# Scaling attention weights on GpSimd and placing the compression units one unit later in a two-layer trunk

## The chip, the core and the metric

The kernel runs on one core of a Trainium2 chip. The metric is the device time of one execution in microseconds. The engines of a core are named as in the profile: PE (TensorE, matrix products and transposes), DVE (VectorE), ACT (ScalarE), POOL or Pool (GpSimd) and SP (SyncE, which issues the transfers from memory).

## What is computed

A trunk of two layers over 256 positions of width 1,024. Each layer adds three branches to the stream. The first mixes positions: eight query heads of width 64 in two groups attend to keys in three ways (compressed blocks, selected blocks, a sliding window), and beside them runs a retention with four heads. The other two are an MLP and a gated input.

```python
def nsa_mixer(q_in, kc_in, vc_in, ks_in, vs_in, kw_in, vw_in, gate_logits, ...):
    q = rmsnorm(q_in.reshape(B, S, G, Hg, dh).transpose(0, 2, 3, 1, 4), qn_g)
    ...
    k_cmp = rmsnorm(compress(k_c, pos_k, w1_k, w2_k), kn_g)
    v_cmp = compress(v_c, pos_v, w1_v, w2_v)
    ...
        p_cmp = masked_softmax(s, cmp_end[None, :] <= t[:, None])
        o_cmp = jnp.einsum('bghqn,bgnd->bghqd', p_cmp.astype(dtype), v_cmp)
    ...
        return gc[..., 0:1] * o_cmp + gc[..., 1:2] * o_slc + gc[..., 2:3] * o_win

def reference(x, p, ...):
    for i in range(DEPTH):
        h = rmsnorm(x, norm_mix[i])
        z = h @ w_in[i]
        ...
        y_a = nsa_mixer(...) @ w_up_nsa[i]
        y_b = retention(rq, rk, rv, rg) @ w_up_ret[i]
        mix = jax.nn.sigmoid(merge_a) * y_a + jax.nn.sigmoid(merge_b) * y_b
        x = x + mix @ w_out[i]
        h = rmsnorm(x, norm_mlp[i])
        x = x + jnp.square(jax.nn.relu(h @ w_ff1[i])) @ w_ff2[i]
        gate = jax.nn.sigmoid(rmsnorm(x, norm_ple[i]) @ w_ple_gate[i])
        x = x + gate * (p[i] @ w_ple[i])
    return x
```

With 256 positions all blocks are selected, so the selected branch is a full causal attention.

## The kernel before

**Units of weight.** A layer's weights come in 142 units of 128 partitions by 1,024 numbers (512 KB). The string ORDER names the first 45 of them in the order in which PE uses them: kcvc and ksvs (keys and values), kvg (window keys, values and gates), q, rq, rk, rv, rg (retention), and w0 to w7 (the first matrix of the compressor). `fa` and `fb` stand for the two halves of the row norm. `_plan` adds the merge, output, MLP and gate units. SP loads each unit into a ring of four buffers `raw`; the units w lie in four other buffers. ACT rounds a unit to its high half `hi` (line 188), and DVE subtracts to get the low half `lo` (line 192). Both have six buffers, and a unit is split four units before its use (AHEAD = 4). PE multiplies three times: high by high, high by low, low by high. One unit is 24 matmuls of 128x256 or 12 of 128x512; a unit w is four matmuls of 128x512.

**Order.** PE's order is that of the program text. Between the matmuls of a unit the program pokes generators (`kv_tail`, `q_tail`, `compress`, `attend` with `softmax` and `scores`, `collect` with `weigh` and `retain`), which emit their instructions when a model clock `vt` says that their inputs should be there. `charge` advances that clock by costs written in the code: for Pool 0.14 us and a microsecond for every 310 elements of a row (a pow: 1.1 or 2.6). A generator yields the model time at which it wants to go on. The order of DVE, ACT and Pool follows a scheduler's priorities. A change in any cost therefore moves instructions on all engines.

**Front of a layer.** `windows` builds the overlapping windows ZB of the compressor's input (DVE `zt`, `zs`, ACT and DVE `ZB`); w0 to w7 multiply them into one accumulator `ot`. `compress` then applies a selection matmul (`pt<-cst,tmp`), a gelu and the second matrix. `kv_tail` norms and transposes keys into KT, `q_tail` transposes the queries into qT and computes the query factor `nq`, minus the product of the row norm `r` and the rsqrt of the head's squares (a pow on Pool, `rso`). All transposes and small products share two buffers `pt`.

**Attention.** Four times (group g, half t), `softmax` takes the scores `sc` of four heads through a mask operation on DVE (line 208, which multiplies by `nq`), an exponential on ACT and the factor `acf` (gate over sum). `weigh` multiplies each block of `e` by its column of `acf` on DVE (`scale`: two or four blocks of 4x128, one of 4x16), transposes the block on PE (`turn`, `pt<-cst,e`), splits it into `pp` or, for the narrow block, PC, and multiplies by V into the single buffer `ot` (`apply`). The last product is `ot<-PC,VC`. ACT and DVE then fold `ot` into `o`, and split that into NHh and NHl, which the units ua multiply. `retain` uses the same buffer `ot` for retention, takes the result through a pow on Pool, and transposes the normed rows (`pt<-cst,tmp`).

Of the kernel before, what the change touches and what calls it, by code (L numbers as in the profile page):

```python
# [12 lines left out]
ALU = mybir.AluOpType  # L13
AX = mybir.AxisListType

P = 128
# [6 lines left out]
NH = 8  # L23
# [22 lines left out]
for _n, _w in PAR_PARTS:  # L46
# [7 lines left out]


ORDER = (
# [4 lines left out]
)  # L61


# [31 lines left out]
def trunk(ctx: ExitStack, tc: tile.TileContext, xT, wu, wg, cst, msk, par, pin, out):  # L95
# [50 lines left out]
    vt = {"pe": 0.0, "act": 0.0, "dve": 0.0, "pool": 0.0}  # L146
    cur = [0.0]

    def width(ap):
        n = 1  # L150
        for d in ap.shape[1:]:
            n *= d
        return n
# [5 lines left out]
    def charge(eng, us):  # L159
        us += 0.03  # L160
        if first[0]:
            cur[0] += us + 0.6
            return
        gs = gaps[eng]
        while len(gs) > 1 and gs[0][1] < vt["pe"] - 6.0:
            gs.pop(0)
        for i, (a, e) in enumerate(gs):
            s = max(a, cur[0])
            if s + us <= e:
                new = []  # L170
                if s - a > 0.15:
                    new.append([a, s])
                if e - s - us > 0.15:
                    new.append([s + us, e])
                gs[i:i + 1] = new
                break
        vt[eng] = gs[-1][0]
        cur[0] = s + us + 0.06

    def fresh(t=None):  # L180
        cur[0] = vt["pe"] if t is None else t
# [27 lines left out]

    def gp(**k):  # L210
        n = width(k["out"])
        charge("pool", (1.1 if n <= 4 else 2.6) if k["op"] == ALU.pow else 0.14 + n / 310)
        return nc.gpsimd.tensor_tensor(**k)  # L213

# [156 lines left out]
    LB = 7.0  # L371
    SL = 0.0
    DE = 0.5
    SLACK = {"kv_tail": 4.0, "q_tail": 3.0, "compress": 0.3, "attend": 1.0, "collect": 0.0}

    def spawn(gen, paced=False):
# [1 line left out]

    def step(gen):
        fresh()  # L380
        if gen.__name__ == "compress":
            first[0] = True
            try:
                with tc.high_priority():
                    d = next(gen)
            finally:
                first[0] = False
        else:
            d = next(gen)
        if d == "now":  # L390
            return cur[0]
        return (cur[0] if d is None else d) + SLACK.get(gen.__name__, SL)

# [125 lines left out]
    def layer(l, st):  # L519
# [108 lines left out]
        def q_tail(t, pq):  # L628
            pv = pq.rearrange("p (h d) -> p h d", h=NH)
            qn = qns[:, t]  # L630
            sq = tmp([P, NH, DH])
            with tc.high_priority():
                act(qn[:, :, 0, :].bitcast(F32R), pv, AF.Copy)
                sub(qn[:, :, 1, :], pv, qn[:, :, 0, :])
                act(sq, pv, AF.Square, scale=r[:, t:t + 1])
            due = cur[0]
            ss = small([P, NH], "qss")
            reduce_sum(ss, sq)
            rs = rsqrt_rows(ss, P, NH, 1.0 / DH)
            pow_due = cur[0]  # L640
            yield due
            yield
            for hh in range(2):
                pt = p_tile([P, 4, P])
                for h in range(4):
                    flip(pt[:, h, :], qn[:, 4 * hh + h].rearrange("p a b -> p (a b)"),
                                        ident)
                act(qT[:, 4 * hh:4 * hh + 4, t * P:(t + 1) * P], pt, AF.Copy)
                if hh == 0:
                    yield vt["pe"]  # L650

            fresh(max(pow_due, vt["pe"]))
            ts(out=nq[:, t], in0=rs, scalar1=r[:, t:t + 1], scalar2=-1.0, op0=ALU.mult, op1=ALU.mult)
            done.add(("q", t))


# [40 lines left out]
        def weigh(g, t):  # L697
# [11 lines left out]

            def scale(i):  # L710
                o, w, b, _ = blocks[i]
                tt(out=e[:, :, o:o + w], in0=e[:, :, o:o + w],
                   in1=cf[:, :, b:b + 1].to_broadcast([P, HG, w]), op=ALU.mult)

            def turn(i):
# [16 lines left out]
                mm(ot, vv, ph.rearrange("p a b -> p (a b)"), start=i == 0, stop=False)  # L732
                mm(ot, vv, pl.rearrange("p a b -> p (a b)"), start=False, stop=i == n)

            fin = []
            scale(0)
            scale(1)
            yield cur[0] + 1.5
            turn(0)
            fin.append(cur[0])  # L740
            yield vt["pe"]
            for i in range(1, n + 1):
                if i < n:
                    fresh(vt["pe"])
                    scale(i + 1)
                fresh()
                turn(i)
                fin.append(cur[0])
                yield fin[i - 1]
                apply(i - 1)  # L750
# [152 lines left out]
                act(ZB[:, :, s, 0, :], zs[:, s, :, :], AF.Copy)  # L903
                sub(ZB[:, :, s, 1, :], zs[:, s, :, :], ZB[:, :, s, 0, :].bitcast(F32))

        r = rh = rr = RB = None
        gk = small([P, 1], "gk")
        todo = set()

# [11 lines left out]
        for name, u in SEQ[l]:  # L921
# [7 lines left out]
            elif name == "fa":  # L929
                finish_a(st)  # L930
                r = st["r"]
                rh = small([P, 2], "rh")
                ts(out=rh, in0=r, scalar1=0.5, scalar2=None, op0=ALU.mult)
                rr = small([P, 2], "rr")
                tt(out=rr, in0=r, in1=r, op=ALU.mult)
                ready("fa")
# [382 lines left out]
```

## Time and profile before

| | us |
|---|---|
| three runs | 866.30, 864.49, 866.05 |
| median of the runs | 866.05 |
| the profiled execution | 865.38 |
| its span in the profile | 863.5 |
| PE busy in the span | 844.8 |
| DVE, ACT, Pool busy | 614.3, 500.7, 37.2 |

The span runs from the first to the last instruction of the profiled execution; the other 1.9 us of that execution lie around it. An engine's busy time says how much of the span it worked; idle time of an engine that nobody waits for costs nothing. Layer 0 takes about the first half of the span. Its front lies between about 20 and 75 us, its attention between 85 and 168 us; in layer 1 the front begins near 445 us and attention ends near 592 us.

### The profile page before, as it was taken

Reading aid. Unit: us, or ns where it says so; the run is one execution under the profiler, and the core shown is the slowest. Engines: PE = TensorE matmul, PEld = TensorE weight load, DVE = VectorE, ACT = ScalarE, POOL = GpSimd, SP = SyncE. Lnnn points to the kernel's source line nnn. Section 1 sums busy time; section 2 is a strip of 40 time slices with the busy share of each in tenths; the row PEclk is TensorE's granted clock in tenths of the full one; section 3 lists DMA queues with packets and bytes.
Section 4 is the critical chain, followed back from the end, with each engine's and each line's share of the span. In section 5 each row is a group of like instructions: output and inputs, shape, how many; then the busy total and the mean of one; then the engine's idle time right before and its main releaser. Section 6 shows DMA issues by size and latency. Waiting matters only on the chain.

```text
span 863.5 us, 16468 instructions
## 1 busy us (share of the span) xinstructions
PE 844.8 (98%) x6647; PEld 817.0 (95%) x6647; DVE 614.3 (71%) x1011; ACT 500.7 (58%) x836; POOL 37.2 (4%) x32
## 2 busy tenths in 40 slices
PE   8999999999999999999999999999999999999997
PEld 7888899899999999999998889998999999999997
DVE  6898897776955555557789879885968555555584
ACT  6786877444744444446576868663556444444461
POOL 1220000000000000000004000000000000000000
PEclk9999999999999999999999999999999999999999
DMA  7867354446556566566665644543556556556541
GB/s 256 314 224 228 123 163 134 137 126 187 190 177 187 183 192 178 190 183 220 188 197 169 200 144 146 172 139 100 158 178 195 178 190 180 187 185 183 194 123 49
DMA packets 44283, 152.10 MB, mean 176 GB/s; under 512 B 5168, under 2 KB 6960, under 8 KB 44208
## 3 DMA queue, kind: packets, MB, share of 16 engines
q1 hardware_dynamic: 44064, 151.04, 55.6%
q8 instruction: 52, 0.85, 0.4%
q14 instruction: 23, 0.19, 0.1%
q10 hardware_dynamic: 144, 0.01, 0.0%
HBM read 149.99 MB, written 1.05 MB: 175 GB/s over the span
## 4 chain that ended last, share of the span: by engine, by line
PE 87%; DVE 7%; ACT 2%; DMA 1%; issue 1%; POOL 1%; SPq 0%; DVEq 0%; ACTq 0%; POOLq 0%
PE mm L219 51%; PE sc L219 16%; PE pt L219 14%; PE ot L219 4%; DVE lo L192 3%; PE pt L224 3%; DMA raw<-in_wu_dram 1%; ACT hi L188 1%; POOL rso L213 1%; DVE zt L192 1%; DVE zs L192 0%; DVE gz L200 0%; DVE XT L192 0%; DVE qn L192 0%; DVE XL L200 0%
## 5 line engine op out<-in xcount | busy, mean ns | idle before, releaser
L192 DVE TENSOR_TENSOR lo<-raw,hi 128x1024 fp32r<-128x1024 f32 (+2 forms) x287 | 342.4, 1198 | 187.3 <-ACT hi L188 186.5
L188 ACT ACTIVATE hi<-raw 128x1024 fp32r<-128x1024 f32 (+2 forms) x287 | 296.4, 1039 | 278.9 <-PE mm L219 164.7
L219 PE MATMUL mm<-XH,hi 128*128 128x256 f32 x992 | 283.3, 286 | 0.0
L219 PE MATMUL mm<-XH,lo 128*128 128x256 f32 x992 | 279.6, 282 | 0.4 <-DVE lo L192 0.4
L219 PE MATMUL mm<-XL,hi 128*128 128x256 f32 x992 | 279.2, 281 | 0.0
L219 PEld LDWEIGHTS mm<-XH,hi 128*128 128x128 f32 x992 | 186.9, 188 | 0.9
L219 PEld LDWEIGHTS mm<-XL,hi 128*128 128x128 f32 x992 | 187.0, 188 | 0.6
L219 PEld LDWEIGHTS mm<-XH,lo 128*128 128x128 f32 x992 | 186.9, 188 | 0.6 <-DVE lo L192 0.6
L219 PE MATMUL sc<-ho,hi 128*128 128x256 f32 x512 | 96.8, 282 | 0.0
L219 PE MATMUL pt<-ho,hi 128*128 128x256 f32 x512 | 96.6, 281 | 0.0
L219 PEld LDWEIGHTS pt<-ho,hi 128*128 128x128 f32 x512 | 78.6, 188 | 0.0
L219 PEld LDWEIGHTS sc<-ho,hi 128*128 128x128 f32 x512 | 78.6, 188 | 0.0
L219 PE MATMUL pt<-ho,lo 128*128 128x256 f32 x256 | 72.0, 281 | 0.0
L219 PE MATMUL sc<-ho,lo 128*128 128x256 f32 x256 | 72.0, 281 | 0.0
L219 PEld LDWEIGHTS sc<-ho,lo 128*128 128x128 f32 x256 | 48.2, 188 | 0.0
L219 PEld LDWEIGHTS pt<-ho,lo 128*128 128x128 f32 x256 | 48.2, 188 | 0.0
L219 PE MATMUL mm<-hi,XH 128*128 128x512 f32 (+2 forms) x128 | 44.7, 349 | 0.0
L219 PE MATMUL mm<-lo,XH 128*128 128x512 f32 (+2 forms) x128 | 43.7, 341 | 0.2 <-DVE lo L192 0.2
L219 PE MATMUL mm<-hi,XL 128*128 128x512 f32 (+2 forms) x128 | 43.7, 341 | 0.0
L188 ACT ACTIVATE e<-e,nmx 128x128 f32<-128x128 f32 (+2 forms) x96 | 37.7, 396 | 9.1 <-DVE nmx L208 8.9
L213 POOL TENSOR_TENSOR rso<-rsv,mhalf 128x2 f32<-128x2 f32 (+3 forms) x18 | 28.2, 1576 | 289.8 <-DVE rsv L196 289.8
L208 DVE CUSTOM_DVE_ANT_0 e<-sc,masks,nq 128x128 f32<-128x128 f32 (+2 forms) x96 | 29.5, 351 | 1.6 <-PE sc L219 1.0
(189 smaller groups left out, 1333.0 us busy)
## 6 DMA issues: line engine op xcount, KB each, us to landing
raw<-in_wu_dram SPq DMA_DIRECT2D x275, 512.0 KB, 3.6
raw<-in_wg_dram SPq DMA_DIRECT2D x8, 280.0 KB, 4.2
cst<-in_cst_dram SPq DMA_DIRECT2D x1, 768.0 KB, 8.1
out_dram<-XT SPq DMA_DIRECT2D x3, 256.0 KB, 2.4
XT<-in_xT_dram SPq DMA_DIRECT2D x4, 128.0 KB, 2.8
raw<-in_wu_dram SPq DMA_DIRECT2D x4, 128.0 KB, 3.0
XT<-in_xT_dram SPq DMA_DIRECT2D x2, 256.0 KB, 6.5
tmp<-in_pin_dram SPq DMA_DIRECT2D x2, 256.0 KB, 3.7
```

The source lines that it names most:

```text
L188: return nc.scalar.activation(o, *a, **k)
L192: return nc.vector.tensor_tensor(**k)
L208: return nc.vector.tensor_tensor_reduce(**k)
L213: return nc.gpsimd.tensor_tensor(**k)
L219: return nc.tensor.matmul(o, a, b_, **k)
L224: return nc.tensor.transpose(o, a, i)
```

## The change

Four things. In ORDER each unit rq0 to rq3 moves ahead of the two units w that stood before it, in both layers. `scale` becomes a Pool multiply, and `weigh` issues all of them at its start; each `turn` is placed when the model has its scale done plus 3 us, where before the first turn came 1.5 us after two scales and each later one after the next scale. In `q_tail` the factor nq is a Pool multiply right behind the pow, by `rn`, which is minus `r` and a new small DVE operation at `fa`; before it was a DVE operation behind the transposes. The list AHEAD_OF_SPLITS names the generator that was named in the code before.

```diff
--- before.py
+++ after.py
@@ -54,10 +54,10 @@
 ORDER = (
-    "kcvc0 kvg0 kvg1 q0 sq kcvc1 kvg2 fa kvg3 q1 fb q2 q3 ksvs0 ksvs1 w0 w1 rq0 w2 w3 rq1 w4 w5  "
-    "rq2 w6 w7 rq3 rk0 rk1 rk2 rk3 rv0 rv1 rv2 rv3 rg0 rg1 rg2 rg3",
+    "kcvc0 kvg0 kvg1 q0 sq kcvc1 kvg2 fa kvg3 q1 fb q2 q3 ksvs0 ksvs1 rq0 w0 w1 rq1 w2 w3  "
+    "rq2 w4 w5 rq3 w6 w7 rk0 rk1 rk2 rk3 rv0 rv1 rv2 rv3 rg0 rg1 rg2 rg3",
...
@@ -637,7 +639,8 @@
             ss = small([P, NH], "qss")
             reduce_sum(ss, sq)
             rs = rsqrt_rows(ss, P, NH, 1.0 / DH)
-            pow_due = cur[0]
+
+            gp(out=nq[:, t], in0=rs, in1=rn[:, t:t + 1].to_broadcast([P, NH]), op=ALU.mult)
             yield due
             yield
             for hh in range(2):
@@ -648,9 +651,6 @@
                 act(qT[:, 4 * hh:4 * hh + 4, t * P:(t + 1) * P], pt, AF.Copy)
                 if hh == 0:
                     yield vt["pe"]
-
-            fresh(max(pow_due, vt["pe"]))
-            ts(out=nq[:, t], in0=rs, scalar1=r[:, t:t + 1], scalar2=-1.0, op0=ALU.mult, op1=ALU.mult)
             done.add(("q", t))
@@ -709,7 +709,7 @@
 
             def scale(i):
                 o, w, b, _ = blocks[i]
-                tt(out=e[:, :, o:o + w], in0=e[:, :, o:o + w],
+                gp(out=e[:, :, o:o + w], in0=e[:, :, o:o + w],
                    in1=cf[:, :, b:b + 1].to_broadcast([P, HG, w]), op=ALU.mult)
@@ -732,17 +732,17 @@
                 mm(ot, vv, ph.rearrange("p a b -> p (a b)"), start=i == 0, stop=False)
                 mm(ot, vv, pl.rearrange("p a b -> p (a b)"), start=False, stop=i == n)
 
-            fin = []
-            scale(0)
-            scale(1)
-            yield cur[0] + 1.5
+            fin, scaled = [], []
+            t0 = cur[0]
+            for i in range(n + 1):
+                fresh(t0)
+                scale(i)
+                scaled.append(cur[0] + 3.0)
+            yield scaled[0]
             turn(0)
             fin.append(cur[0])
-            yield vt["pe"]
             for i in range(1, n + 1):
-                if i < n:
-                    fresh(vt["pe"])
-                    scale(i + 1)
+                yield scaled[i]
                 fresh()
                 turn(i)
                 fin.append(cur[0])
...
@@ -931,6 +931,8 @@
                 r = st["r"]
                 rh = small([P, 2], "rh")
                 ts(out=rh, in0=r, scalar1=0.5, scalar2=None, op0=ALU.mult)
+                rn = small([P, 2], "rn")
+                ts(out=rn, in0=r, scalar1=-1.0, scalar2=None, op0=ALU.mult)
                 rr = small([P, 2], "rr")
                 tt(out=rr, in0=r, in1=r, op=ALU.mult)
                 ready("fa")
```


PE runs 5,791 rows in both programs, DVE 946 before and 923 now, Pool 38 and 58. The rows below give engine, operation and operands in the order in which an engine runs them; a number behind a name tells buffers of that name apart, and "..." stands for rows left out.

PE, layer 0, from the end of ksvs1 (`mm_493`) to rq0. Before, `hi_429` and `hi_452` are w0 and w1, `mm_600` is rq0:

```order
L219 MATMUL mm_493<-hi_393,XL_103 128x256
L219 MATMUL ot_580<-hi_429,ZB_166 128x512
L219 MATMUL ot_580<-lo_430,ZB_166 128x512
...
L219 MATMUL ot_580<-hi_452,ZB_166 128x512
...
L224 MATMUL pt_595<-cst,tmp_372 128x128 x2
L219 MATMUL mm_600<-XH_102,hi_496 128x256
```

There rq0 stands behind both units w and a pair of key transposes. Now `hi_431` is rq0, `hi_454` and `hi_500` are w0 and w1:

```order
L220 MATMUL mm_497<-hi_395,XL_103 128x256
L220 MATMUL mm_578<-XH_102,hi_431 128x256
...
L220 MATMUL mm_578<-XH_102,lo_432 128x256
L225 MATMUL pt_603<-cst,tmp_372 128x128 x2
...
L220 MATMUL ot_620<-hi_454,ZB_166 128x512
L220 MATMUL ot_620<-lo_455,ZB_166 128x512
...
L220 MATMUL ot_620<-hi_500,ZB_166 128x512
...
L225 MATMUL pt_635<-cst,tmp_383 128x128 x2
```

The 24 matmuls of rq0, with a pair of key transposes among them, now stand between ksvs1 and w0, and the other pair of transposes behind w1.

DVE, layer 0, first weighing, from the last mask operation of its fourth head. `e_1064`, `acf_1121` belong to this softmax, `e_1125` to the next:

```order
L208 ISA e_1064,nmx_1065<-sc_1112,masks,nq_170 128x128
...
L196 TENSOR_SCALAR acf_1121<-smx_1066 128x12
L693 RECIPROCAL acf_1121<-acf_1121 128x12
L192 TENSOR_TENSOR acf_1121<-acf_1121,gates_161 128x12
L192 TENSOR_TENSOR e_1064<-e_1064,acf_1121 128x4x128 x2
L208 ISA e_1125,nmx_1126<-sc_1156,masks,nq_170 128x256
...
L192 TENSOR_TENSOR lo_1144<-raw_1029,hi_1143 128x1024
...
L192 TENSOR_TENSOR e_1064<-e_1064,acf_1121 128x4x16
```

There acf and two multiplies follow the mask operations at once. Now (`e_1087` and `acf_1148` belong to this softmax, `e_1152` to the next):

```order
L208 ISA e_1087,nmx_1088<-sc_1139,masks,nq_170 128x128
...
L208 ISA e_1152,nmx_1153<-sc_1174,masks,nq_170 128x256
...
L196 TENSOR_SCALAR acf_1148<-smx_1089 128x12
L208 ISA e_1152,nmx_1153<-sc_1177,masks,nq_170 128x256
...
L693 RECIPROCAL acf_1148<-acf_1148 128x12
L192 TENSOR_TENSOR acf_1148<-acf_1148,gates_161 128x12
L192 TENSOR_TENSOR lo_1195<-raw_1072,hi_1194 128x1024
L192 TENSOR_TENSOR lo_1243<-raw_1115,hi_1242 128x1024
L192 TENSOR_TENSOR pp_1210<-pt_1204,pp_1209 128x512
```

The multiplies by acf have left DVE, two mask operations of the next softmax stand in front of the end of acf, and two low halves behind it.

Pool, layer 0, from the first query pow to the second weighing, now; before, of these rows only those of `rso` were Pool's:

```order
L214 TENSOR_TENSOR rso_482<-rsv_480,mhalf 128x8
L214 TENSOR_TENSOR nq_170<-rso_482,rn_341 128x8
L214 TENSOR_TENSOR rso_493<-rsv_491,mhalf 128x8
L214 TENSOR_TENSOR nq_170<-rso_493,rn_341 128x8
L214 TENSOR_TENSOR rso_566<-rsv_564,mhalf 128x2
...
L214 TENSOR_TENSOR e_1087<-e_1087,acf_1148 128x4x128 x2
L214 TENSOR_TENSOR e_1087<-e_1087,acf_1148 128x4x16
L214 TENSOR_TENSOR e_1152<-e_1152,acf_1293 128x4x128 x4
L214 TENSOR_TENSOR e_1152<-e_1152,acf_1293 128x4x16
```

Each nq stands behind its pow and ahead of the next one, and the pows of the keys (128x2) behind them.

PE, layer 0, end of the last weighing. Before, `mm_1999` is a merge unit, `mm_2121` the first unit ua:

```order
L219 MATMUL ot_1866<-pp_2051,V_160 128x512
L219 MATMUL mm_1999<-XH_102,hi_1877 128x256
...
L219 MATMUL mm_1999<-XH_102,lo_1878 128x256
L219 MATMUL ot_1866<-PC,VC 128x512 x2
L219 MATMUL mm_2121<-NHh_162,hi_1911 128x256
...
L219 MATMUL ot_2146<-rV_171,rs_1865 128x128 x4
```

There the merge unit ends ahead of the last product, and ua runs 18 of its matmuls, the last six of which need the second group's NHh, before retention. Now `mm_2028` is a merge unit, `mm_2142` the first unit ua:

```order
L220 MATMUL ot_1861<-pp_2047,V_160 128x512
...
L220 MATMUL ot_1861<-PC,VC 128x512 x2
L220 MATMUL mm_2028<-XH_102,hi_1886 128x256
...
L220 MATMUL mm_2028<-XH_102,lo_1887 128x256
L220 MATMUL ot_2120<-rV_171,rs_1873 128x128 x4
L220 MATMUL mm_2142<-NHh_162,hi_1936 128x256
...
L220 MATMUL ot_2155<-rV_171,rs_1873 128x128 x4
```

Behind the last `ot<-PC,VC` now stand 18 matmuls of the merge unit and three groups of retention matmuls (`ot<-rV`) with 12 matmuls of ua among them, before ua reaches the second group's NHh in its third block of six; before, the 12 matmuls of ua stood there alone.

## Rows read from the trace of the kernel before

**Rows 1.** The page, part 1: busy us, share, instructions.

```profile
PE 844.8 (98%) x6647; PEld 817.0 (95%) x6647; DVE 614.3 (71%) x1011; ACT 500.7 (58%) x836; POOL 37.2 (4%) x32
```

**Rows 2.** Waits of PE: us in total, times, longest us.

```profile
PE mm L219 <- ACT NHh L188: 3.2, 2, 1.6
PE ot L219 <- DVE ZB L192: 3.2, 2, 1.6
...
PE pt L224 <- DVE tmp L200: 1.0, 2, 0.6
```

**Rows 3.** Timeline, front of the layers (start, us, engine, line, operation, idle before):

```profile
40.53 0.50 PE L219 MATMUL ot<-hi,ZB 128*128 128x512 f32 x1 [1.60 <-DVE ZB L192]
...
43.55 0.39 PE L219 MATMUL mm<-XH,lo 128*128 128x256 f32 x1 [0.44 <-DVE lo L192]
...
49.63 0.66 PE L224 MATMUL pt<-cst,qn 128*128 128x128 f32 x4 [0.69 <-ACT qT L188]
...
38.06 1.21 DVE L192 TENSOR_TENSOR lo<-raw,hi 128x1024 fp32r<-128x1024 f32 x1
39.20 1.28 DVE L192 TENSOR_TENSOR ZB<-zs,ZB 128x512 fp32r<-128x512 f32 x2
...
42.28 1.21 DVE L192 TENSOR_TENSOR lo<-raw,hi 128x1024 fp32r<-128x1024 f32 x1
...
487.04 0.63 PE L219 MATMUL pt<-cst,tmp 128*128 128x64 f32 x4 [1.19 <-DVE KT L200]
```

**Rows 4.** Timeline, layer 0, end of the last weighing, PE, then ACT, then DVE.

```profile
167.83 0.63 PE L219 MATMUL ot<-PC,VC 128*128 128x512 f32 x2
168.30 0.28 PE L219 MATMUL mm<-NHh,hi 128*128 128x256 f32 x1
168.42 0.28 PE L219 MATMUL mm<-NHl,hi 128*128 128x256 f32 x1
...
171.50 0.38 PE L219 MATMUL mm<-NHh,hi 128*128 128x256 f32 x1 [1.62 <-ACT NHh L188]
171.96 0.39 PE L219 MATMUL mm<-NHl,hi 128*128 128x256 f32 x1
...
169.00 0.77 ACT L188 ACTIVATE o<-ot 64x256 f32<-64x256 f32 x2
...
171.03 0.42 ACT L188 ACTIVATE NHh<-o 128x256 fp32r<-128x256 f32 x1 [0.61 <-DVE o L192]
...
170.15 0.85 DVE L192 TENSOR_TENSOR o<-ot,o 64x256 f32<-64x256 f32 x2
```

**Rows 5.** Windows: us, busy us (instructions), granted clock, DMA share, GB/s.

```profile
core 0: us, PE busy (x) PEld busy (x) DVE busy (x) ACT busy (x) POOL busy (x), PEclk, DMA share, GB/s
85.00:165.00 80.00, 80.00 (x592) 74.92 (x591) 68.09 (x183) 59.21 (x154) 0.00 (x0) 1.00 0.45 141
165.00:175.00 10.00, 8.30 (x65) 7.68 (x64) 5.34 (x8) 4.70 (x8) 0.00 (x0) 1.00 0.35 106
590.00:600.00 10.00, 8.30 (x53) 7.72 (x52) 4.02 (x8) 4.02 (x8) 0.00 (x0) 0.84 0.32 105
```

**Rows 6.** Timeline of DVE, first weighing; a group of all: busy, mean ns.

```profile
88.63 0.35 DVE L208 CUSTOM_DVE_ANT_0 e<-sc,masks,nq 128x128 f32<-128x128 f32 x1
...
90.62 0.17 DVE L192 TENSOR_TENSOR acf<-acf,gates 128x12 f32<-128x12 f32 x1
...
L208 DVE CUSTOM_DVE_ANT_0 e<-sc,masks,nq 128x256 f32<-128x256 f32 x32 | 15.3, 479 | 0.5
```

**Rows 7.** A DVE group; timeline of Pool, and of DVE beside it.

```profile
L192 DVE TENSOR_TENSOR e<-e,acf 128x512 f32<-128x512 f32 x24 | 15.6, 686 | 0.1
...
1.87 0.95 POOL L534 MEMSET zs<- 128x1024 f32 x1
...
29.66 1.60 POOL L213 TENSOR_TENSOR rso<-rsv,mhalf 128x2 f32<-128x2 f32 x1 [0.62 <-DVE rsv L196]
...
233.50 0.70 POOL L213 TENSOR_TENSOR r<-ms,mhalf 128x2 f32<-128x2 f32 x1 [49.63 <-DVE ms L196]
...
469.55 7.48 POOL L213 TENSOR_TENSOR rso<-rsv,mhalf 128x2 f32<-128x2 f32 x2 [1.35 <-DVE rsv L196]
...
471.12 3.48 DVE L192 TENSOR_TENSOR lo<-raw,hi 128x1024 fp32r<-128x1024 f32 x3
```

More of the change, by code (lines that the diff above doesn't have):

```diff
@@ L211, in gp @@
         n = width(k["out"])
+        assert k["op"] in (ALU.pow, ALU.mult, ALU.add)
         charge("pool", (1.1 if n <= 4 else 2.6) if k["op"] == ALU.pow else 0.14 + n / 310)
@@ L373, in trunk @@
     DE = 0.5
+    AHEAD_OF_SPLITS = ("compress",)
     SLACK = {"kv_tail": 4.0, "q_tail": 3.0, "compress": 0.3, "attend": 1.0, "collect": 0.0}
@@ L380, in step @@
         fresh()
-        if gen.__name__ == "compress":
+        if gen.__name__ in AHEAD_OF_SPLITS:
             first[0] = True
@@ L904, in windows @@
                 sub(ZB[:, :, s, 1, :], zs[:, s, :, :], ZB[:, :, s, 0, :].bitcast(F32))
-        r = rh = rr = RB = None
+        r = rh = rr = rn = RB = None
         gk = small([P, 1], "gk")
```

4 rows, old and new, of the table ORDER are left out of this document.

## Prediction

> **What bounds the kernel now.** The first view is the page's list of engines: TensorE (PE) is busy 844.8 of 863.5 us [rows 1], so a change can only pay by taking away PE's stalls or PE's work, and this one leaves PE the same 5,791 rows in another order. The second view is the list of what PE waited for [rows 2]: a few waits, each of which comes once per layer or so. The third is PE's own order of time at those places. In layer 0 the first compression unit w0 waits 1.60 us for the windows ZB, rq0 then waits 0.44 us for a low half, and the query flips wait 0.69 us; in layer 1 the compressor's selection matmul waits 1.19 us for KT [rows 3]. Behind the last weighing PE waits 1.62 us for NHh, and the next matmul comes at 171.96 instead of 171.62, since its NHl is 0.34 us later still [rows 4]. Layer 1 repeats ZB and NHh at 1.6 us each [rows 2]. The flips of the normed retention rows wait 1.0 us in two goes [rows 2].
>
> The windows view adds one thing. In the 10 us that hold the NHh stall, both layers lose the same busy time, but layer 1 does 53 matmuls against 65 and its granted clock is 0.84 against 1.00 [rows 5]: the clock fell there, after the stall. A 128x256 matmul starts 0.12 us after the one before it (168.30 to 168.42), a 128x512 one 0.235 us (two from 167.83 to 168.30) [rows 4]; 12 matmuls are 1.4 us. Between, in the whole of attention (85 to 165 us), PE is busy 80.00 of 80 us, though VectorE (DVE) is busy 68.09 [rows 5].
>
> So the ceiling is: layer 0 1.60 + 0.44 + 0.69 + 1.62 + 0.34 + 0.60 = 5.3; layer 1 1.60 + 1.19 + 1.62 + 0.34 + 0.40 + 1.40 = 6.5; together **11.8 us**. Restarts after the other stalls, about 0.1 us each, are not counted.
>
> **The change part by part.**
>
> *Scales leave DVE.* 24 multiplies at 0.686 us [rows 7], 8 small ones and 4 factors nq leave DVE: some 18 us of DVE work over both layers. I cost this at **nothing** for PE: where these stand PE has no stall [rows 5], because the splits run four units ahead (AHEAD = 4, a unit is 24 x 0.12 = 2.9 us, so some 11 us). That lead also hides it if Pool should hold up DVE: 12 wide and 4 narrow multiplies in a layer.
>
> *rq0 in front of w0.* 24 matmuls of 0.12 us = 2.9 us now lie between ksvs1 and w0. w0 was ready to start 1.60 us early, so in both layers the ZB stall goes, provided rq0's own low half is there: w0's and w1's were, and rq0 now comes earlier in DVE's queue than they do. What is late next: w1. In layer 0 its low half is the third from ksvs1 and takes the place of the one that ends at 43.49 (42.28 + 1.21 [rows 3]). PE would reach w1 0.93 us after w0's start, that is at 40.53 - 1.60 + 2.86 + 0.22 (a pair of flips now stands ahead) + 0.93 = 42.9; I leave **0.5** there (0 to 1.0). The query flips in layer 0 wanted buffers that were late by 0.69; they now come 0.6 us later than before on PE's clock without stalls, but behind a low half that is as late; I leave 0.3 (0 to 0.7). In layer 1 I leave 0.4 for them, where the list shows no such wait. The 1.19 us for KT in layer 1: KT's turn on DVE moves behind one more rope operation (0.7 us, as wide as a scale), while PE's selection moves from 485.85 to about 489 (rq3 is now in front of w6 and w7, and 2.9 us are between). KT's last operation would be done near 488, so the stall goes; I leave 0.2 in each layer (0 to 1.2 in layer 1). SyncE's queue now brings rq0 before w0 and w1, which lie in other buffers; no one waits for that.
> Front, left over: 0.5 + 0.3 + 0.2 in layer 0, 0.4 + 0.2 in layer 1: **1.6 us**.
>
> *End of the last weighing.* The supply runs from the last ot<-PC (end about 168.3) over ACT's o (169.00), DVE's o (170.15 + 0.85) and NHh (171.03 + 0.42) to 171.5: 3.2 us, of which PE had 12 matmuls, 1.43 us, to cover [rows 4]. In the new order 18 matmuls of a merge unit (2.1 us), three groups of four retention matmuls (some 0.44 us each) and 12 of the next unit (1.4 us) stand between: 4.9 us against 3.2. The stall goes, and the clock had no stall to fall after. What is late next: the first retention group writes the single buffer ot, which o must have been read from; o is done 2.0 to 2.7 us after PC, PE asks after 2.1. I leave 0.2 each: **0.4**.
>
> *Flips of the normed rows.* They stood 0.60 and 0.40 us early; three matmul groups are moved around them, and I halve it: **0.5** left (0 to 1.0).
>
> *Price of Pool's multiplies.* Only the first weighing of a layer is tight. By the order, PE turns to its first flips after 9 + 12 matmuls of 128x512 and four score matmuls, 5.4 us after head 3's scores; the second block's flips follow 2.3 us, the third's (16 wide) 2.8 us later. Before, the factor acf was done at 90.79, 1.8 us behind head 3's last mask operation [rows 6]. Now two mask operations of 0.48 us of the next softmax and their scores (four matmuls, 0.5 us) stand in front: 1.1 us for head 3's own mask operations + 1.8 + 2 x 0.48 + part of the 0.5 put acf some 4.2 us behind head 3's scores. That leaves 1.2 us for the first 512-wide multiply, 3.5 for two, 6.3 for all. No row shows a Pool multiply of that width. From below: filling 1,024 columns took Pool 0.95 us, so 0.5 for a single pass over 512 [rows 7]. From above in an ordinary case: a pow of two columns, 0.70 us when DVE is idle, took 1.60 us beside a low half on DVE [rows 7]; with three passes of 0.5 and one such delay of 0.9 a multiply takes 2.4, and DVE's next two operations there are low halves. The loss, max(p - 1.2, 2p - 3.5) for p us each, lies between 0 and 1.3 us, and 2.3 if two low halves come back to back; I take **1.0 per layer, 2.0 together**, as the delayed row is the nearer one. The weighings after it have over 4 us of room at each flip, by the same counting.
>
> The Trainium skill, GPSIMD Engine Reference, section 3.1, gives 4497 ns for a Pool tensor_tensor over 2,048 fp32 columns; an estimate from that page is 1.1 us for 512, and by it alone the 2.0 would be 0 and the time 856.1. No run here shows it.
>
> *nq on Pool.* Four multiplies of 8 columns, 0.70 to 1.6 us each by the same rows, stand ahead of the pows of the keys. They delay the rotated keys' factor by 1 to 3 us; its flips come 8 us later. Cost 0; without that cover at most 1 us.
>
> **Sum.** 11.8 - (1.6 + 0.4 + 0.5 + 2.0) = 7.3 us. On the profiled execution's 865.4 us that gives **858.1**; its time lies 0.7 us under the median of the runs, 866.05, within their spread, and I name 858. With all left-overs at their lower end 853.7; with Pool at 2.3 per layer, 1.0 at w1, 1.2 at KT and the flips unmended, 862.6.
>
> **Rivals.**
>
> *The stalls only move.* The front of a layer is bound by DVE's queue, so what PE doesn't wait for at w0 it waits for at w1, the query flips and KT; and the clock falls once more. For it: the 0.44 and 0.69 us stalls follow the ZB stall within 10 us [rows 3]. Against: rq0 gives DVE 2.9 us once and the queue isn't longer. Then the front saves 2.5 instead of 3.9 us, the clock's 1.4 stays lost, and Pool may take 0.9 more: 858.1 + 1.4 + 1.4 + 0.9 = about 862, at most 864.
>
> *Pool eats the gain.* p about 3.2 in both first weighings (2.9 us each, 5.8 in place of 2.0) and the retention flips as before: 858.1 + 3.8 + 0.5, and with the clock's 1.4 still lost 863.8; with p = 3.8, 866. The change then moves nothing that can be measured.
>
> *Slower: Pool starves behind DVE.* Two pows of two columns together took 7.48 us from 469.55, while DVE ran three low halves without a gap (3.48 us from 471.12) and more behind them [rows 7]: the second alone took over 5 us. Low halves took 1.16 us each all the while, so it is Pool that waits. If a 512-wide multiply behind two low halves takes p = 5.8 us, both first weighings lose 2p - 3.5 = 8.1 us: 865.4 - 11.8 + 2.5 + 16.2 = 872. The change is slower by over 0.2% from p = 4.7. Against it: at this place mask operations, which read one operand from PSUM, stand between the low halves, and DVE has just lost the multiplies.
> The Trainium skill, SBUF — State Buffer, section Who interferes with whom, says that a DVE instruction with two SBUF inputs and a Pool instruction that reads SBUF exclude each other, whichever came first holding the ports to its end. The trace agrees for the pows (0.70 against 1.60 us); by that rule alone Pool would get in after each low half, and p stays under 3.
>
> **How the numbers follow.** Chances: forecast 0.60 (its own range 854 to 862.5), stalls move 0.15 (862 to 864), Pool eats the gain 0.11 (864 to 867.5), slower 0.10 (868 to 875), more than forecast 0.04. The range 854 to 865 takes in the first two and a third of the third: 0.8. A measurement of this kernel can tell about 0.2%, 1.7 us, from no change; so faster (under 864.3) 0.79, same 0.11, slower 0.10.
>
> **What would show it.** In the profile after: no wait of ot for ZB and none of mm for NHh, granted clock 1.00 in the 10 us behind layer 1's last weighing, selection in layer 1 without its 1.2 us; a new wait of pt for e on Pool of about 1 us, twice, and Pool's 512-wide multiplies at 1 to 2.4 us. I am wrong if that wait is over 3 us, if waits for low halves in the 20 us behind ksvs1 add up to more than 3 us, or if NHh is still waited for.

## The result, and the profile after

The changed kernel takes 859.28 us (median; 858.74 to 860.14) against 865.95 for the kernel before; the ratio is 0.9927, with a 95% interval from 0.9910 to 0.9944. It is faster, and 1.3 us slower than the 858.0 forecast. The span of its profiled execution is 857.3 us, 6.2 less than before.

The page, part 1, of the changed kernel answers to [rows 1]. PE runs the same 6,647 matmuls; DVE has 11.7 us less, Pool 41 us more:

```profile
PE 842.5 (98%) x6647; PEld 816.4 (95%) x6647; DVE 602.6 (70%) x977; ACT 500.1 (58%) x836; POOL 78.6 (9%) x68
```

What PE waited for (us in total, times, longest us), answering to [rows 2]; the lines left out are start-up and the front:

```profile
PE ot L220 <- ACT tmp L188: 1.7, 2, 0.9
...
PE ot L220 <- DVE PC L192: 1.5, 2, 0.8
...
PE pt L225 <- POOL e L214: 1.2, 2, 0.6
PE sc L220 <- DVE nmx L208: 0.7, 2, 0.5
```

ZB, NHh and the flips of the normed rows are gone from the list. In their place stand ACT's `tmp` (retention), DVE's PC, Pool's `e` and DVE's `nmx`, each twice, that is once per layer. (The diff adds lines to the file, so that line 219 of before is line 220 here, and 224 is 225.)

PE's timeline (start, us, engine, line, operation, idle before it) at the places of [rows 3, 4]: the front of layer 0 (w1, the query flips), then the new stalls of layer 0 in the order of time (the first flips of attention, the narrow block of the third weighing, retention), then the selection in layer 1:

```profile
43.15 0.50 PE L220 MATMUL ot<-lo,ZB 128*128 128x512 f32 x1 [0.43 <-DVE lo L192]
...
49.11 0.66 PE L225 MATMUL pt<-cst,qn 128*128 128x128 f32 x4 [0.49 <-DVE KT L200]
...
95.23 0.66 PE L225 MATMUL pt<-cst,e 128*128 128x128 f32 x4 [0.62 <-POOL e L214]
...
144.87 0.50 PE L220 MATMUL ot<-PC,VC 128*128 128x512 f32 x1 [0.74 <-DVE PC L192]
...
170.76 1.16 PE L220 MATMUL ot<-rV,rs 128*128 128x128 f32 x8 [0.85 <-ACT tmp L188]
...
485.56 0.63 PE L220 MATMUL pt<-cst,tmp 128*128 128x64 f32 x4 [0.38 <-DVE KT L200]
```

The windows view (us, then busy us of each engine, granted clock) for attention and for the 10 us behind each layer's last weighing, answering to [rows 5]. PE is no longer busy all through attention (78.48 of 80 us, before 80.00), and the clock behind layer 1's last weighing is 1.00, not 0.84:

```profile
core 0: us, PE busy (x) PEld busy (x) DVE busy (x) ACT busy (x) POOL busy (x), PEclk, DMA share, GB/s
85.00:165.00 80.00, 78.48 (x581) 73.66 (x581) 62.35 (x166) 58.07 (x154) 18.73 (x16) 1.00 0.43 133
165.00:175.00 10.00, 9.15 (x76) 8.85 (x75) 6.48 (x14) 5.87 (x11) 1.01 (x1) 1.00 0.43 138
590.00:600.00 10.00, 9.15 (x79) 8.94 (x78) 6.73 (x13) 5.89 (x10) 2.86 (x2) 1.00 0.36 122
```

### The profile page after: what moved, and what is told of

The parts are those of the page before. It is cut to its first block, busy times and chain, and to the rows that moved or that the text cites. A ratio compares the mean times of both kernels' runs of the same rounds, so it can differ in the third digit from the quotient of the medians.

```text
span 857.3 us, 16518 instructions
## 1 busy us (share of the span) xinstructions
PE 842.5 (98%) x6647; PEld 816.4 (95%) x6647; DVE 602.6 (70%) x977; ACT 500.1 (58%) x836; POOL 78.6 (9%) x68
## 3 DMA queue, kind: packets, MB, share of 16 engines
HBM read 149.99 MB, written 1.05 MB: 176 GB/s over the span
## 4 chain that ended last, share of the span: by engine, by line
PE 86%; DVE 6%; ACT 4%; DMA 1%; issue 1%; POOL 1%; SPq 0%; DVEq 0%; ACTq 0%; POOLq 0%
PE mm L220 49%; PE sc L220 17%; PE pt L220 14%; PE ot L220 4%; PE pt L225 2%; DVE lo L192 2%; ACT e L188 1%; ACT hi L188 1%; DMA raw<-in_wu_dram 1%; DVE e L208 1%; POOL e L214 0%; DVE o L192 0%; DVE zt L192 0%; ACT tmp L188 0%; ACT T L188 0%
## 5 line engine op out<-in xcount | busy, mean ns | idle before, releaser
L214 POOL TENSOR_TENSOR e<-e,acf 128x512 f32<-128x512 f32 (+1 forms) x32 | 37.4, 1198 | 110.2 <-ACT hi L188 40.0
```

## The experiments

Times are medians, and each ratio is to the kernel before on the same chip (865.2 to 865.6 us). The experiments ran on three chips, so a few tenths of a microsecond between two experiments say nothing. The changed kernel stands at 859.3.

| kernel | units | scales done by | places of turns | us |
|---|---|---|---|---|
| before | old | DVE | old | 865.2 to 866.0 |
| e1 | new | DVE | old | 863.55 |
| e2 | old | Pool | later | 859.39 |
| changed | new | Pool | later | 859.28 |
| e3 (nq on DVE) | new | Pool | later | 859.39 |
| e10 | new | Pool | old | 856.63 |
| e4 | new | DVE | as changed | 863.25 |
| e11 | old | Pool | as before | 866.41 |
| e12 | new | DVE | as e10 | 854.80 |
| e13 | old | DVE | old, Pool's charge | 861.26 |
| e8, e9 | new | Pool | attention 1 us earlier, later | 866.30, 870.25 |
| e14 | w1 later | Pool | old | 861.16 |
| e7 | new | Pool, twice | as changed | 869.07 |

**The parts alone.** First the order of the units alone (layer 0's string of the two):

```diff
-ksvs0 ksvs1 w0 w1 rq0 w2 w3 rq1 w4 w5 rq2 w6 w7 rq3
+ksvs0 ksvs1 rq0 w0 w1 rq1 w2 w3 rq2 w4 w5 rq3 w6 w7
```

> The kernel before with nothing but the new place of rq0 to rq3 ahead of the units w. Theory A (the gain is where PE's matmuls stand): the ZB, query-flip and selection stalls of both layers go as in the changed kernel, 3.2 to 1.3 us in layer 0 and 3.4 to 0.5 us in layer 1, some 4.8 us; the NHh stall of 1.6 us per layer and the lower clock behind layer 1's stay; attention has no stall. About 861. Theory B (the gain is DVE's relief): nothing has left DVE, so 865 to 866.

Measured: 863.55 us, ratio 0.9973 (0.9964 to 0.9983). PE's waits in that kernel:

```profile
PE mm L219 <- DVE RHl L192: 1.6, 2, 0.8
PE mm L219 <- ACT NHh L188: 1.5, 2, 0.8
...
PE ot L219 <- ACT PC L188: 1.3, 2, 0.7
...
PE ot L219 <- DVE PC L192: 0.7, 2, 0.4
```

The front gained what theory A named (no ZB, no query wait for qT). Part of it was given back: attention's pieces fell elsewhere, and behind the last weighing PE now waits for PC (1.3 and 0.7), for RHl, the low half of the normed retention rows (1.6), and still for NHh (1.5). The time lies between theory A's 861 and theory B's 865.

Then the scales on Pool with the later turns alone:

```diff
-                tt(out=e[:, :, o:o + w], in0=e[:, :, o:o + w],
+                gp(out=e[:, :, o:o + w], in0=e[:, :, o:o + w],
...
-            scale(0)
-            scale(1)
-            yield cur[0] + 1.5
...
+            for i in range(n + 1):
+                fresh(t0)
+                scale(i)
+                scaled.append(cur[0] + 3.0)
+            yield scaled[0]
...
-                if i < n:
-                    fresh(vt["pe"])
-                    scale(i + 1)
+                yield scaled[i]
```

> The kernel before with the scales on Pool and the later turns, and nothing else. Theory A: the ZB, query and selection stalls stay (6.6 us); the order puts 18 merge matmuls behind the last ot<-PC as in the changed kernel, so the NHh stall and the clock's loss go (some 5.6 us with the retention wait of about 1.0 per layer that replaces it: 3.6 net) and the flips of the normed rows gain 1.3; attention gets the changed kernel's waits of about 2.2 us per layer. Sum about -0.5: 865. Theory B: the whole relief of DVE but nq is here, so nearly the whole gain: 860.

Measured: 859.39 us, 0.9924 (0.9902 to 0.9946). This part alone has nearly the whole gain. Its waits, but for those of start-up, which every kernel has:

```profile
PE ot L219 <- DVE ZB L192: 3.8, 2, 2.1
...
PE pt L219 <- DVE KT L200: 1.1, 1, 1.1
...
PE pt L224 <- ACT qT L188: 0.7, 1, 0.7
```

The front stalls are all there, and nothing else is: attention, the end of the last weighing and retention run without a wait. Theory A had put the changed kernel's attention waits here, and they belong to the two parts together. The time is theory B's, but this run changes the engine and the turns at once and doesn't tell which of them gains. The gains of 1.6 and 5.8 us do not add: with both parts it is 6.7, and 5.8 on this chip in the next run, which has both but for nq.

Then nq back on DVE:

```diff
-            gp(out=nq[:, t], in0=rs, in1=rn[:, t:t + 1].to_broadcast([P, NH]), op=ALU.mult)
+            pow_due = cur[0]
...
+            fresh(max(pow_due, vt["pe"]))
+            ts(out=nq[:, t], in0=rs, scalar1=r[:, t:t + 1], scalar2=-1.0, op0=ALU.mult, op1=ALU.mult)
```

> The changed kernel with nq back on DVE behind the query flips. PE's order is the same. Theory A: nq is off the path, 859.3 within 0.5. Theory N (nq on Pool matters, by delaying the keys' pows or by freeing DVE): over 0.7 us away, with the wait at the query flips or at KT changed.

Measured: 859.39 us, with the same span of 857.3 us. nq is off the path, as theory A said.

**The engine and the place, apart.** The planner's charge sets the places; the engine that does the work can be chosen without it. In four kernels one was held and the other changed. Where the engine alone differs (the changed kernel and e4, the kernel before and e11, e10 and e12), the traces have all 6,647 matmuls of PE in the same order. First the places of the changed kernel, with DVE at work:

```diff
-                gp(out=e[:, :, o:o + w], in0=e[:, :, o:o + w],
-                   in1=cf[:, :, b:b + 1].to_broadcast([P, HG, w]), op=ALU.mult)
+                charge("pool", 0.14 + HG * w / 310)
+                eng = nc.vector
+                eng.tensor_tensor(out=e[:, :, o:o + w], in0=e[:, :, o:o + w],
+                                  in1=cf[:, :, b:b + 1].to_broadcast([P, HG, w]), op=ALU.mult)
```

> The changed kernel with the scales issued on DVE at the same places; PE's order is the same as in the changed kernel. Theory A: the placement carries the gain and Pool only costs: the waits for Pool's e (0.79 us per layer with the restart) go, those for nmx behind NHl (0.3 and 0.7) too, the retention wait stays; some 2.5 us faster than the changed kernel, 857. Theory B: DVE has its 17 us back, its low halves come late in attention: 862 or more, with PE waits for lo or pp.

Measured: 863.25 us, 0.9985 (0.9972 to 0.9999): 4.0 us slower than with Pool. Theory B's time holds here, but the wait is not the one it named: PE waits for nmx, the mask operations' last output, and not for low halves or `pp`. The largest waits, and DVE's timeline where the first arises in layer 0:

```profile
PE sc L220 <- DVE nmx L208: 4.7, 2, 2.4
...
PE ot L220 <- ACT tmp L188: 1.7, 2, 0.9
PE ot L220 <- DVE PC L192: 1.5, 2, 0.8
...
107.14 1.29 DVE L714 TENSOR_TENSOR e<-e,acf 128x512 f32<-128x512 f32 x2
...
108.68 1.42 DVE L714 TENSOR_TENSOR e<-e,acf 128x512 f32<-128x512 f32 x3
110.02 0.69 DVE L200 SCALAR_TENSOR_TENSOR rG<-tmp,rG 128x512 f32<-128x512 f32 x1
110.74 0.35 DVE L208 CUSTOM_DVE_ANT_0 e<-sc,masks,nq 128x128 f32<-128x128 f32 x1
...
111.67 0.48 PE L220 MATMUL sc<-KT,qT 128*128 128x272 f32 x2 [2.37 <-DVE nmx L208]
```

Five scales of the second weighing (1.29 and 1.42 us) and `rG` stand ahead of the next softmax's mask operations, so the score buffers come free 2.4 us late, in each layer. The waits for PC and for retention's `tmp` stay as with Pool, so Pool has no part in those. At these places, then, the 5.9 us by which the changed kernel beats the one before are 1.9 by the places and 4.0 by Pool. No low half takes over 1.24 us here, so it is the place in DVE's queue that costs, and not a slower DVE.

Then the places of the kernel before, with Pool at work:

```diff
-                tt(out=e[:, :, o:o + w], in0=e[:, :, o:o + w],
-                   in1=cf[:, :, b:b + 1].to_broadcast([P, HG, w]), op=ALU.mult)
+                charge("dve", 0.07 + HG * w / 960)
+                nc.gpsimd.tensor_tensor(out=e[:, :, o:o + w], in0=e[:, :, o:o + w],
+                                        in1=cf[:, :, b:b + 1].to_broadcast([P, HG, w]), op=ALU.mult)
```

> The kernel before with its scales issued on Pool at their old places, the planner charging DVE for them as before; PE's order is that of the kernel before. Theory R (freeing DVE is worth nothing where PE doesn't wait for it, and the gain needs the new places): the front stalls, NHh and the normed flips stay, attention has no wait, as acf is done 3.3 us ahead of its first flips and a Pool scale takes 1.04 us; 865 within 1. Theory E (the engine is what gains): DVE and ACT get ahead everywhere and NHh comes earlier; 862 or less.

Measured: 866.41 us, 1.0010 (0.9999 to 1.0022): nothing gained, so theory E falls. NHh costs exactly what it did, and attention has no wait, as theory R said:

```profile
PE ot L219 <- DVE ZB L192: 3.6, 2, 1.9
PE mm L219 <- ACT NHh L188: 3.2, 2, 1.6
...
PE pt L224 <- DVE tmp L200: 0.9, 2, 0.5
```

The granted clock doesn't hide a gain. It fell in more places of the profiled execution than before, but executions with the same mean clock, 0.996, took 865.7 to 867.1 us, and 865.6 to 867.5 with the kernel before.

Then old turns (two scales, first turn 1.5 us behind, each later scale with the turn before it), with rq first and Pool at work:

```diff
-            for i in range(n + 1):
-                fresh(t0)
-                scale(i)
-                scaled.append(cur[0] + 3.0)
-            yield scaled[0]
...
+            scale(0)
+            scale(1)
+            yield cur[0] + 1.5
...
-                yield scaled[i]
+                if i < n:
+                    fresh(vt["pe"])
+                    scale(i + 1)
```

> The changed kernel with the old placing of the turns: two scales, then the first turn 1.5 us after, each later scale issued as the turn before it is placed, all on Pool. Theory A: the flips of the first weighing stand closer behind its scale but the planner charges Pool 1.8 us for a scale that takes 1.04, so flips wait 0.5 to 1.5 us in each weighing of half 0 and less in half 1; 860 to 863. Theory L (the later turns are what makes Pool's scales affordable): waits for Pool's e of over 1 us in every weighing, 866 or more.

Measured: 856.63 us, 0.9891 (0.9865 to 0.9917), 2.7 us better than the changed kernel and better than either theory said. PE's list has no wait for Pool at all: the 3 us that the change adds ahead of each turn aren't needed for Pool's sake.

The same places with DVE at work:

```diff
-                gp(out=e[:, :, o:o + w], in0=e[:, :, o:o + w],
-                   in1=cf[:, :, b:b + 1].to_broadcast([P, HG, w]), op=ALU.mult)
+                charge("pool", 0.14 + HG * w / 310)
+                nc.vector.tensor_tensor(out=e[:, :, o:o + w], in0=e[:, :, o:o + w],
+                                        in1=cf[:, :, b:b + 1].to_broadcast([P, HG, w]), op=ALU.mult)
```

> The kernel with rq first, old turns and Pool's charges (856.6 with Pool), with the scales issued on DVE; PE's order is the same as there. Theory R: DVE is not what attention waits for, 856.6 within 1. Theory E: in places planned for a free DVE the 17 us of scales make mask operations and splits late, as they did at the places of the changed kernel (863.25 against 859.3): 860 or more, with waits of sc for nmx or of ot for pp.

Measured: **854.80 us**, 0.9878 (0.9861 to 0.9894), the fastest of all, with nothing scaled on Pool. Its list of waits, but for start-up:

```profile
PE pt L225 <- DVE KT L200: 0.7, 2, 0.5
PE mm L220 <- DVE NHl L192: 0.4, 2, 0.2
PE pt L220 <- DVE KT L200: 0.4, 1, 0.4
```

It is below both theories: R had 856.6 within 1, E 860 or more. DVE does the scales 1.8 us faster here than Pool (1.4 us when each is set against the kernel before on its own chip). With Pool, PE waits 0.28 us for `pp` in each layer, and here it doesn't; the rest of the difference wasn't assigned.

Last, the kernel before with only the charge changed:

```diff
-                tt(out=e[:, :, o:o + w], in0=e[:, :, o:o + w],
-                   in1=cf[:, :, b:b + 1].to_broadcast([P, HG, w]), op=ALU.mult)
+                charge("pool", 0.14 + HG * w / 310)
+                nc.vector.tensor_tensor(out=e[:, :, o:o + w], in0=e[:, :, o:o + w],
+                                        in1=cf[:, :, b:b + 1].to_broadcast([P, HG, w]), op=ALU.mult)
```

> The kernel before with one number changed in the planner: a scale is charged to Pool (1.8 us at 128x512) where before it was charged to DVE (0.6), while DVE still does it. Units, turns and nq are those of before. Theory R (the gain is where the planner puts the pieces): the front stalls stay (some 7 us); the NHh stall, the lower clock behind it and the waits of the normed flips go or change; 859 to 863. Theory E (the gain needs the work off DVE): no better than before, 865 or more, since PE's front is the same and DVE does what it did.

Measured: 861.26 us, 0.9952 (0.9935 to 0.9968). Units, the rule for the turns, nq and engine are those of before; one cost in the planner gave 4.2 us, as theory R said. The list has neither NHh nor the normed flips any more, ZB is shorter, and retention's `tmp` and attention's `e` and nmx are new:

```profile
PE ot L219 <- DVE ZB L192: 2.3, 2, 1.2
...
PE ot L219 <- ACT tmp L188: 1.1, 2, 0.6
...
PE pt L224 <- DVE e L713: 0.7, 2, 0.4
```

**Another fall of the pieces.** The changed kernel with attention's start moved:

```diff
-            yield vt["pe"] + 1.5
+            yield vt["pe"] + 0.5
```

> The changed kernel with one number changed: attention may begin 0.5 us after its inputs in the planner's clock instead of 1.5, so scores, flips and products land between other matmuls. Theory P (attention's 4.4 us of waits and the 2.0 us at retention in the changed kernel come from where its pieces fell between the units; the Pool-only kernel had none of them): most of the 6.4 us go, the front stays, 853 to 856. Theory Q (they come from the compression units standing later, which leaves attention less time): they stay, 859 within 1.

Measured: 866.30 us, 1.0008 (0.9993 to 1.0023). Theory P had expected the best here. Attention lost all but 0.6 us of its waits, but the stretch behind the last weighing got worse ones:

```profile
PE mm L220 <- DVE RHl L192: 2.4, 2, 1.2
PE mm L220 <- ACT RHh L188: 2.1, 2, 1.1
PE mm L220 <- ACT NHh L188: 2.0, 2, 1.0
```

All of PE's waits together are only 2.6 us longer than in the changed kernel. The granted clock was lower behind the new ones of layer 0 (0.90 and 0.93 in the 10 us from 180 and from 190 us, 1.00 in the changed kernel); how much of the 7.0 us that is was not worked out.

The other way:

```diff
-            yield vt["pe"] + 1.5
+            yield vt["pe"] + 2.5
```

> The same number at 2.5 instead of 1.5. Theory P: another fall of the pieces, with the end of the last weighing closer packed; waits of another kind, anywhere between 853 and 862, and not those of the changed kernel. Theory Q: 859 within 1, or a microsecond worse, as attention ends later.

Measured: 870.25 us, 1.0047 (1.0032 to 1.0061), outside theory P's band as well as Q's: waits on `pp` (2.2 us in all), `e` (1.7), `rs`, RHl (1.6 each) and NHh (1.5) in place of the changed kernel's, 5.7 us more in all; the other half of the 11.0 us wasn't assigned. One microsecond in the planner's clock, with all the work the same, costs 7.0 us one way and 11.0 the other. Theory Q (less time for attention) falls with e8 and e10, where the units stand as in the changed kernel and attention's waits went; of theory P the direction stands, but not its numbers.

The units once more, with w1 a unit later:

```diff
-ksvs0 ksvs1 rq0 w0 w1 rq1 w2 w3 rq2 w4 w5 rq3 w6 w7
+ksvs0 ksvs1 rq0 w0 rq1 w1 w2 rq2 w3 w4 rq3 w5 w6 w7
```

> The same kernel (rq first, old turns, Pool) with the units as rq0 w0 rq1 w1 w2 rq2 w3 w4 rq3 w5 w6 w7, so that w1 has 2.9 us more. The wait for w1's low half (0.65 us) goes. If attention falls as before: 855 to 856. If its pieces fall otherwise (theory P), any value from 852 to 865, read from the waits behind 85 us.

Measured: 861.16 us, 0.9952 (0.9936 to 0.9968), 4.5 us slower than e10, from which it differs in the units alone. PE now waits for rq1's low half instead of w1's, and the selection for KT up to 1.5 us; attention's end fell otherwise, too.

**The price of a Pool multiply.** Each scale followed by a second one:

```diff
+                nc.gpsimd.tensor_tensor(out=e[:, :, o:o + w], in0=e[:, :, o:o + w],
+                                        in1=ones.unsqueeze(2).to_broadcast([P, HG, w]), op=ALU.mult)
```

> The changed kernel with every Pool scale followed by a second Pool multiply of the same width, by one; PE's order is the same. A scale alone took 1.04 us at 128x512 in the changed kernel, so two take 2.1, and 3.0 behind a low half. Theory A (only the first weighing of a layer is tight for Pool, since what it waits for is acf and one low half): its flips come 1.0 to 1.5 us later per layer, the other weighings have room for 5 us; DVE's low halves are held up a microsecond more here and there. 861.5 to 863.5. Theory S (Pool's share of the port holds DVE so that the mask operations and low halves come late): the waits for nmx grow from 0.3 and 0.7 to over 2 us, 866 or more.

Measured: 869.07 us, 1.0038 (1.0027 to 1.0049), 9.8 above the changed kernel: outside theory A's 861.5 to 863.5, and in theory S's band, though not by its wait. Only the first weighing of a layer pays, by 3.6 us in place of 0.6. Pool's timeline there, PE's first flips, and the window around them:

```profile
93.03 2.92 POOL L214 TENSOR_TENSOR e<-e,acf 128x512 f32<-128x512 f32 x2 [18.09 <-DVE acf L192]
95.91 3.02 POOL L714 TENSOR_TENSOR e<-e,ones 128x512 f32<-128x512 f32 x2
...
97.98 0.33 PE L225 MATMUL pt<-cst,e 128*128 128x128 f32 x1 [3.59 <-POOL e L714]
...
95.00:105.00 10.00, 7.02 (x33) 5.96 (x34) 5.30 (x10) 3.44 (x11) 4.48 (x5) 0.83 0.36 107
520.00:530.00 10.00, 6.41 (x28) 5.06 (x27) 4.65 (x10) 3.56 (x9) 5.92 (x6) 0.83 0.38 107
```

The order put both scales ahead of both second multiplies, so the first flips wait for three Pool operations. The waits give 6.0 us of the 9.8; the granted clock fell to 0.83 in the windows that hold these stalls, in both layers. How much of the other 3.8 us that is wasn't worked out. Theory S's mechanism falls: the wait for nmx is 0.2 us in all.

## Why the prediction was right

The forecast was 858.0, and 859.28 came; the sign and the size of the gain were right, and so were the stalls that went. That it came within 1.3 us is in part luck, as the sum below shows. Term by term, in idle time of PE as the waits give it:

- **Ceiling 11.8 us**: those stalls are gone or shrunk as listed, and the clock stayed at 1.00 behind the last weighing, as I had said.
- **Front, 1.6 left**: 0.43 (w1) + 0.49 (query flips, on KT) + 0.38 (selection in layer 1) = 1.3. Right; e1, without Pool, has 1.35 there, in part at other places.
- **Normed flips, 0.5 left**: 0.
- **Pool, 2.0**: 0.62 + 0.62 = 1.2. The mechanism was as put: acf done at 93.09, a low half on DVE from 93.04, and Pool's first multiply beside it took 1.93 us instead of 1.04. By the prediction's formula that is 1.93 - 1.2 = 0.73; my middle value of 2.4 for a multiply was too dear.
- **End of the last weighing, 0.4 left**: 1.7. The step named the wrong reader. The first retention group found `ot` free; the second must wait until ACT has copied the first group's result out of the same buffer, which stands behind a high half and a tanh:

```profile
168.14 1.05 PE L220 MATMUL ot<-rV,rs 128*128 128x128 f32 x8
...
168.22 1.06 ACT L188 ACTIVATE hi<-raw 128x1024 fp32r<-128x1024 f32 x1
169.50 0.63 ACT L188 ACTIVATE T<-z 128x512 f32<-128x512 f32 x1 [0.23 <-DVE z L192]
170.03 0.67 ACT L188 ACTIVATE tmp<-ot,r 128x512 f32<-128x512 f32 x1
```

  The wait for NHh went, with more cover than I had counted: without the stall PE had 6.4 us of work between the last `ot<-PC` and the second group's NHh, not 4.9, since a group of retention runs as eight matmuls in 0.8 us and I had put 0.44. What failed is that I followed `ot` only to its first new writer.
- **"The weighings after it have over 4 us of room"**: for Pool's multiplies this holds; no other flips wait for `e`. But attention lost 2.2 us that the sum has no term for: PC, 0.75 per layer, and nmx, 0.7 in all. The first is queue order: ACT's PC comes behind a high half, DVE's behind a low half:

```profile
141.93 1.04 ACT L188 ACTIVATE hi<-raw 128x1024 fp32r<-128x1024 f32 x1
142.87 0.57 ACT L188 ACTIVATE PC<-pt 16x512 fp32r<-16x512 f32 x1
...
143.00 1.22 DVE L192 TENSOR_TENSOR lo<-raw,hi 128x1024 fp32r<-128x1024 f32 x1
144.14 0.67 DVE L192 TENSOR_TENSOR PC<-pt,PC 16x512 fp32r<-16x512 f32 x1
```

  The PC wait costs the same 1.5 us with DVE at work (e4), so it comes from where the flips and the last product fell. The second goes with Pool's multiplies, as far as the trace tells. `NHl`, with two inputs in SBUF, took 0.73 us between them instead of 0.42, with mask operations behind it, and in layer 1 `rG` ahead of it took 1.06 instead of 0.72; the wait there is 0.51 against 0.16. No run tests it by itself, and with twice the multiplies (e7) it is 0.2 in all. `NHl` in layer 0:

```profile
108.30 0.73 DVE L192 TENSOR_TENSOR NHl<-o,NHh 128x256 fp32r<-128x256 f32 x1
```

So three terms were too dear (0.3 + 0.5 + 0.8), one too cheap (1.3), and one was missing (2.2): two mistakes in opposite directions, of 1.6 and 3.5 us, of which a part cancels. By them 7.3 becomes 5.4; the span shows 6.2. Of the 0.8 between, 0.2 lies in the waits of the first 20 us, and the rest wasn't assigned.

**What was right for a reason that needs a limit** is the first step, that DVE's relief is worth nothing to PE. At the places of before it is so (e11, 866.4). At the places of the changed kernel it is worth 4.0 us (e4), because all scales of a weighing now stand ahead of the next mask operations; and at old turns with Pool's charge DVE does it 1.4 to 1.8 us better than Pool (e10, e12). The relief pays only for what the later turns cost. So the gain can't be shared out between engine and place in one way: place first, the change gains 1.9 us with DVE still at work (865.2 to 863.25) and 4.0 more by Pool; engine first, it gains nothing (e11) and the places all the rest. That places alone can gain is shown by e13, where a single charge gives 4.2 us, and by e12, with the most of all and no scale on Pool.

The rivals: "the stalls only move" did not come true as put, since the front has 1.3 us left; but new stalls came elsewhere, 3.4 us in attention (1.2 + 1.5 + 0.7) and 1.7 at retention. "Pool eats the gain" and "Pool starves" did not come true: they needed multiplies of 3.2 and of 4.7 us or more, and the longest of Pool's 32 took 2.05.

## What to carry to other kernels

Where a planner's cost sets the order of a full engine, a change of engine is two changes, and they can be had apart: charge one engine and issue on the other. Here the charge alone gained 4.2 us, and the sign of the engine's part hung on the place. Before a stall is counted as gone, follow the buffer to all of its next writers and their readers; and look for new stalls where there were none, since PE at 80.00 of 80 us says nothing of how near its suppliers were.

## What the runs showed of the hardware

A Pool multiply of 128x512 with two fp32 inputs in SBUF took 1.04 us where DVE was out of the way (16 of the 24, 1.04 to 1.05), against 0.686 on DVE [rows 7], and the 128x64 one 0.30 us. The Trainium skill, GPSIMD Engine Reference, section 3.1, led to an estimate of 1.1 us; the trace agrees. Three in a row (two wide, one narrow) show it below, at 120.75. At 93.25, with a low half begun on DVE at 93.04, three took 4.17 us.

Against what I read from the pows, DVE waits too. Low halves that began behind a Pool multiply took 1.99 and 2.10 us instead of 1.23, in both layers. Low halves of over 1.4 us stand in the trace of every kernel here that scales on Pool, and in none that scales on DVE (before, e1, e4, e12, e13):

```profile
93.25 4.17 POOL L214 TENSOR_TENSOR e<-e,acf 128x512 f32<-128x512 f32 x3 [17.95 <-DVE acf L192]
...
120.75 2.31 POOL L214 TENSOR_TENSOR e<-e,acf 128x512 f32<-128x512 f32 x3 [8.57 <-DVE acf L192]
...
95.27 1.99 DVE L192 TENSOR_TENSOR lo<-raw,hi 128x1024 fp32r<-128x1024 f32 x1 [1.00 <-ACT hi L188]
...
109.91 2.10 DVE L192 TENSOR_TENSOR lo<-raw,hi 128x1024 fp32r<-128x1024 f32 x1
```

The Trainium skill, SBUF — State Buffer, section Who interferes with whom, says that whichever began first holds the ports to its end; the trace agrees in both directions.

The clock does not fall behind every stall of 1.6 us. It fell behind layer 1's NHh stall in the kernel before [rows 5] and not behind layer 0's of the same length; in e2 it fell at the ZB stall of layer 0 (2.1 us; 0.83 from 36 to 46 us), where the 1.60 us of the kernel before left it at 1.00. In e11, with PE's matmuls in the order of the kernel before, the two NHh stalls are again 1.62 us each, and it is layer 0 that has the lower clock (0.83 from 170 to 180 us) while layer 1 has 1.00 from 590 to 600. So the length of the stall doesn't decide it alone, and the 1.4 us for the clock in the prediction's ceiling are a loss of the one execution that was profiled, which need not be in every one. What decides it stays open here.
